# Consecutive weight rows on each partition, and every fourth feature to match, in the expert stage of a hybrid encoder

## The chip, the core and the metric

The kernel runs on one core of one Trainium2 chip. TensorE multiplies matrices, VectorE, ScalarE and GpSimd do the elementwise work, SyncE (SP) issues nearly all DMAs, and 16 DMA engines move the data. The metric is the device time of one execution in microseconds.

## The reference

One encoder layer over 256 tokens of 1024 features in float32: a mixer of three branches (retention, neighbourhood attention, cross attention to a memory), an output projection with a residual, and then a mixture of experts. Only the last part is touched:

```python
t = rmsnorm(x, g_ffn)                      # 256 x 1024
grp = top-1 of 4 groups, exp = top-2 of 4 experts in that group, with weights
for g in range(4):
    a = einsum('td,edf->tef', t, w_gate[g])      # 4 experts, 1024 -> 512
    u = einsum('td,edf->tef', t, w_up[g])
    hid = silu(a) * u * combine[:, g, :, None]
    out += einsum('tef,efd->td', hid, w_down[g]) # 512 -> 1024
y = rmsnorm(x + out, g_final)
```

Each of the 16 experts has 2 MB of gate, 2 MB of up and 2 MB of down weights: some 100 MB, which are read once.

## The kernel before, in words

Ahead of the experts the kernel projects, attends and mixes; TensorE runs products of split pairs (a high and a low part, L128 and L129 make them, L306 to L308 multiply). There a scheduler orders the instructions by its own costs, except those that are pinned in program order (`pin`, `tc.keep_in_program_order`). The small loads for the router stand in this part: its weights `wr` (L727, L728; L730 multiplies them by the gain column `gt[:, 3]`), biases, the constants `iota` and `tri` (L739 casts it) and x. All go through SP's one queue, among the loads of the next weights.

From L796 on the order is written out by hand. The expert weights arrive in slots of 1 MB, [128 partitions, 2048 floats], some 20 of them. `expert_units` makes the list of 96 loads in the order of use. `fetch(tag)` issues the next load into the slot that came free, `take` hands the oldest loaded slot to the matmuls. A load is issued when the last matmul on its slot is done.

The stage runs over 8 pairs of experts; each expert has room for 64 tokens. Every second pair, `gather` picks the tokens of four experts: 32 matmuls, whose stationary operand is a 128-feature slice of the normalised activations (`x1_hi`, then `x1_lo`) and whose moving operand is the 0/1 matrix `pd`. The result, multiplied by the norm gain while it leaves PSUM, is `xg`: feature k*128 + p on partition p of block k. For each expert `gate_up` then takes four slots. Each holds 256 rows of gate (two blocks k) and the same of up, row k*128 + p on partition p, so a row of 512 floats is a run of 2 KB. The matmuls have `xg[:, k]` as stationary and the weights as moving operand, gate into the upper, up into the lower half of a bank. ScalarE and VectorE make `gs` of it (silu times up). `hidden` transposes `gs` in four slices of 128 features, `down` multiplies by the down weights (rows of 1024 floats, runs of 4 KB), `weigh` splits and weighs the result, `scatter` adds it to the tokens' sums in PSUM. The last pair is finished with `down_1`, which takes the down weights by halves of the columns (runs of 2 KB). For the tail, slots that are free by then hold `g_final` and the output.

```python
for h, w in ((0, w_gate), (1024, w_up)):
    rows_in(w[e, r : r + 256])(raw[:, h : h + 1024])       # "(k p) n -> p k n"
```

Of the kernel before, what the change touches and what calls it, by code (L numbers as in the profile page):

```python
# [9 lines left out]
F32 = mybir.dt.float32  # L10
# [4 lines left out]
AF = mybir.ActivationFunctionType  # L15
# [3 lines left out]
P = 128  # L19
T = 256  # L20
D = 1024
KT = D // P
NEG = -1e30
SLOTS = 64
NE = 16
NP = NE // 2
DFF = 512
# [3 lines left out]
def hybrid_encoder_kernel(  # L31
# [31 lines left out]
    nc = tc.nc  # L63
    w_gate = w_gate[0].rearrange("g e d f -> (g e) d f")
    w_up = w_up[0].rearrange("g e d f -> (g e) d f")
    w_down = w_down[0].rearrange("g e f d -> (g e) f d")
    V, A, G, PE = nc.vector, nc.scalar, nc.gpsimd, nc.tensor

    cp = ctx.enter_context(tc.tile_pool(name="cp", bufs=1))
# [19 lines left out]
    pin = tc.keep_in_program_order  # L89
# [18 lines left out]
    def hl_pair(shape):  # L108
        tag = hl_tags.pop(0)
        hl_tags.append(tag)  # L110
        t = slot(tag, [P, 2, *shape], F32R)
        return tag, t[:, 0], t[:, 1]
# [24 lines left out]
    feeder = [nc.sync]  # L137
# [6 lines left out]
        plan.pop(0)(raw)  # L144
        ready.append((tag, raw))

    def rows_in(src, parts=1):
        def go(raw):
            dst = raw.rearrange("p (k n) -> p k n", n=src.shape[1])
            k = dst.shape[1] // parts  # L150
            for i in range(parts):
                feeder[0].dma_start(
                    dst[:, i * k : i * k + k], src[i * k * P : (i + 1) * k * P].rearrange("(k p) n -> p k n", p=P)
                )

        return go

# [15 lines left out]
    gt = cp.tile([P, 4, KT], F32, name="gt")  # L173
# [4 lines left out]
    for q in range(4):  # L178
        rs = slice(q * 256, q * 256 + 256)
# [3 lines left out]
    ident = cp.tile([P, P], F32, name="ident")  # L183
# [72 lines left out]
    with tc.manual_schedule():  # L256
# [4 lines left out]
        for q in range(4):  # L261
            ks = (2 * q, 2 * q + 1)
            gained(xT, 0, hT_hi, hT_lo, ks)
            _, w_hi, w_lo = hl_pair([2, 512])
            for k in ks:
                raw = first[k // 4][:, k % 4]
# [160 lines left out]
    def xa_scores(hp):  # L427
        s = at([P, 4, 256])
        for j in range(2):
            h = 2 * hp + j  # L430
            for a in range(2):
                ts = slice(a * P, (a + 1) * P)
                mm3(s[:, 2 * j + a], xq_hi[:, h, ts], xq_lo[:, h, ts], mk_hi[:, h], mk_lo[:, h], True, True)
        return softmax(s, P ** -0.5)
# [56 lines left out]
    p = xa_scores(0)  # L491
# [11 lines left out]
    def na_scores(hp):  # L503
        sps = at([P, 4, 256])
        for a in range(2):
            ts = slice(a * P, (a + 1) * P)
            for i, (q, k) in enumerate(((nq_hi, nk_hi), (nq_hi, nk_lo), (nq_lo, nk_hi))):
                for j in range(2):
                    rs = slice(j * 64, j * 64 + 64)
                    pin(PE.matmul(sps[:, 2 * j + a], q[rs, hp, ts], k[rs, hp], start=i == 0, stop=i == 2))  # L510
        s = tmp([P, 4, 256])
        mx = tiny(4, tag="mx")
        for j in range(2):
            for a in range(2):
                i = 2 * j + a
                r0 = 2 - 2 * a
                b = bias[2 * hp + j][:, r0 : r0 + 4].rearrange("p r c -> p (r c)")
                V.tensor_tensor_reduce(s[:, i], sps[:, i], b, 0.125, -3e38, ALU.add, ALU.max, accum_out=mx[:, i : i + 1])
        return softmax(s, 1.0, mx)
# [49 lines left out]
    p = na_scores(0)  # L569
    rk_hi, rk_lo = rope_T("C1", proj_T(units_T(W, C_RK, D), hT_hi, hT_lo))  # L570
    ps = na_probs(p)
    p = na_scores(1)
# [13 lines left out]
    p = na_scores(2)  # L586
# [3 lines left out]
    p = na_scores(3)  # L590
# [112 lines left out]
    w = ret_scores(0)  # L703
    rg(0)
    ret_out(0, *w)
    w = ret_scores(1)
# [17 lines left out]
    raw_tags.append("B1")  # L724
    wr = wp.tile([P, KT, 32], F32, tag="gs", name="wr")
    V.memset(wr, 0.0)
    tc.keep_in_program_order(nc.sync.dma_start(wr[:, :, 16:20], w_rg[0].rearrange("(k p) n -> p k n", p=P)))  # L727
    tc.keep_in_program_order(nc.sync.dma_start(wr[:, :, 0:16], w_re[0].rearrange("(k p) n -> p k n", p=P)))  # L728
    for k in range(KT):
# [34 lines left out]
    def expert_units():  # L764
        us = []

        def gate_and_up(e, r):
            def go(raw):
                for h, w in ((0, w_gate), (1024, w_up)):
                    rows_in(w[e, r : r + 256])(raw[:, h : h + 1024])  # L770

            return go

        def gu(e):
            us.extend(gate_and_up(e, r) for r in range(0, D, 256))

        def dn(*es):
            for r in (0, 256):
                us.extend(rows_in(w_down[e, r : r + 256]) for e in es)

        def dn_cols(e):
            for c in (0, 512):
                us.append(rows_in(w_down[e, :, c : c + 512], 2 if c and e == NE - 1 else 1))

        for p in range(NP):
            gu(2 * p)
            if p:
                dn(2 * p - 2, 2 * p - 1)
            gu(2 * p + 1)
        dn_cols(NE - 2)  # L790
        dn_cols(NE - 1)
        return us
# [8 lines left out]
    tag = raw_tags.pop(0)  # L801
# [6 lines left out]
    parts = []  # L808
    for i, (tag, raw) in enumerate(out_raw):
        src = w_out[0, i % 2 * 512 : i % 2 * 512 + 512, i // 2 * 512 : i // 2 * 512 + 512].rearrange("(k p) n -> p k n", p=P)  # L810
        if i < 3:
            nc.sync.dma_start(raw, src)
            raw = [raw[:, :2], raw[:, 2:]]
# [106 lines left out]
    def bank(shape):  # L920
        return psc.tile(shape, F32, tag="b", name=nm("b"))
# [59 lines left out]
    def normed_lo(a, n):  # L981
        ns = slice(n * 512, n * 512 + 512)
        V.scalar_tensor_tensor(
            x1_lo[:, a, ns], x1[:, a, ns], r2[:, a : a + 1], x1_hi[:, a, ns].bitcast(F32), op0=ALU.mult, op1=ALU.subtract
        )
# [130 lines left out]
    def gather(pd, lead=False):  # L1116
        pts = [bank([P, 2, 256]) for _ in range(4)]

        def part(u, x, first):
            for j in range(2):  # L1120
                ks = slice((2 * u + j) * P, (2 * u + j + 1) * P)
                for a in range(2):
                    PE.matmul(
                        pts[u][:, j],
                        x[:, a, ks],
                        pd[:, a].rearrange("p e s -> p (e s)"),
                        start=first and j + a == 0,
                        stop=not first and j + a == 2,
                    )

        if lead:
            for u in range(4):
                part(u, x1_hi, True)
            for n in range(2):
                for a in range(2):
                    normed_lo(a, n)
        xg = slot("C1", [P, KT, 4, SLOTS])
        for u in range(4):
            pt = pts[u]
            if not lead:  # L1140
                part(u, x1_hi, True)
            part(u, x1_lo, False)
            if u % 2:
                for j in range(2):
                    k = 2 * u + j
                    A.activation(
                        xg[:, k].rearrange("p e s -> p (e s)"), pt[:, j], AF.Copy, scale=gt[:, 3, k : k + 1]
                    )
            else:
                V.tensor_tensor(  # L1150
                    xg[:, 2 * u : 2 * u + 2].rearrange("p k e s -> p k (e s)"),
                    pt,
                    gt[:, 3, 2 * u : 2 * u + 2].unsqueeze(2).to_broadcast([P, 2, 256]),
                    op=ALU.mult,
                )
        return xg
# [22 lines left out]
    def take(n):  # L1179
        tag, raw = ready.pop(0)  # L1180
        return tag, raw.rearrange("p (k n) -> p k n", n=n)

    def gate_up(xg, i, p, gs, between=None):
        pt = bank([P, DFF])
        for u in range(2):
            for h in range(2):
                tag, w = take(DFF)
                for j in range(2):
                    k = 4 * u + 2 * h + j
                    for c in range(2):  # L1190
                        PE.matmul(  # L1191
                            pt[c * 64 : c * 64 + 64], xg[:, k, p % 2 * 2 + i], w[:, 2 * c + j], start=k == 0, stop=k == KT - 1
                        )
                fetch(tag)
            if between and not u:
                between()
        gs = gs or keep([P, DFF], "gs")
        A.activation(gs[64:128], pt[0:64], AF.Silu)  # L1198
        V.tensor_mul(gs[i * 64 : i * 64 + 64], gs[64:128], pt[64:128])  # L1199
        return gs  # L1200
# [34 lines left out]
    def hidden(gs, hh=None, i=0):  # L1235
        rs = slice(i * 64, i * 64 + 64) if hh else slice(0, P)
        pt = bank([P, 4, P])
        for j in range(4):
            PE.transpose(pt[:, j, rs], gs[rs, j * P : (j + 1) * P], ident[rs, rs])
        hh = hh or keep([P, 4, P], "hh")  # L1240
        A.copy(hh[:, :, rs], pt[:, :, rs])
        return [hh[:, :, n * 64 : n * 64 + 64] for n in range(2)]
# [43 lines left out]
    def experts(pd, first, lead=False):  # L1286
        st = {}

        def turn():
            st["h"] = hidden(st["gs"])  # L1290
# [135 lines left out]
```

## Time and profile before

| | us |
|---|---|
| median of three runs (545.28 to 545.74) | 545.31 |
| the profiled execution | 545.44 |
| its span in the trace | 543.5 |
| TensorE busy in the span | 528.5 |
| VectorE, ScalarE, GpSimd busy | 264.3, 229.0, 18.5 |

The profile is that of one execution. Its page gives busy times of each engine; a matmul's end in it is modelled, so that pipelined matmuls overlap in the records and their starts say more than their lengths. PE stands for TensorE's matmuls, PEld for its weight loads (the stationary operand), which can run beside a matmul. DVE is VectorE, ACT ScalarE, SPq the queue of SyncE that issues DMAs. In the windows, the first number behind a stretch is its length, then the busy time of each engine with its instructions, the granted clock of TensorE as a share of full speed, the share of time that the 16 DMA engines were busy, and GB/s. The page puts the DMAs at a mean of 294 GB/s over the span, with 89815 packets for 159.91 MB, 89776 of them under 8 KB.

### The profile page before, as it was taken

The numbers are of one execution on the slowest core, as the hardware profiler recorded it, in microseconds if no ns is written. First come the engines' busy times: TensorE is split into PE (matmuls) and PEld (weight loads), VectorE is DVE, ScalarE is ACT, GpSimd is POOL, SyncE is SP. The second block draws the span as 40 slices with busy tenths as digits, with TensorE's granted clock in tenths as the row PEclk, the third lists the DMA queues.
The fourth block names the chain that finished last, engine by engine and source line by source line (L and its number), as shares of the span: only waits on it lengthen the run. The fifth ranks groups of instructions, "written<-read, shape, count | busy, mean of one in ns | idle before, by whom it ended". The sixth has DMA issues, their size and how long they took to land. (4 is left out here: it accounts for less than half of the span.)

```text
span 543.5 us, 7482 instructions
## 1 busy us (share of the span) xinstructions
PE 528.5 (97%) x2912; PEld 359.9 (66%) x2912; DVE 264.3 (49%) x461; ACT 229.0 (42%) x378; POOL 18.5 (3%) x21
## 2 busy tenths in 40 slices
PE   8999999999999999999999999999999999999992
PEld 6999899967778888888888863353435343534340
DVE  6598798995657768384566171130112111210122
ACT  6775566698654464544535261121111111111123
POOL 0005000040000000000000000000000000000000
PEclk9999999999999999999999999999999999999997
DMA  8987778045445799739983799999999999999962
GB/s 302 390 316 233 224 147 256 17 156 163 148 154 189 235 334 301 257 103 403 354 318 151 275 344 330 416 406 418 406 414 409 409 413 407 416 406 418 406 242 81
DMA packets 89815, 159.91 MB, mean 294 GB/s; under 512 B 13104, under 2 KB 27824, under 8 KB 89776
## 3 DMA queue, kind: packets, MB, share of 16 engines
q1 hardware_dynamic: 89056, 158.80, 80.1%
q10 hardware_dynamic: 720, 0.58, 0.3%
q8 instruction: 25, 0.41, 0.3%
q14 instruction: 14, 0.11, 0.1%
HBM read 158.32 MB, written 1.05 MB: 293 GB/s over the span
## 5 line engine op out<-in xcount | busy, mean ns | idle before, releaser
L129 DVE TENSOR_TENSOR h<-r,h 128x1024 fp32r<-128x1024 f32 x58 | 71.2, 1239 | 31.6 <-ACT h L128 31.2
L128 ACT CAST h<-r 128x1024 fp32r<-128x1024 f32 x58 | 60.2, 1048 | 23.4 <-PE pj L308 12.5
L306 PE MATMUL pj<-h,A 128*128 128x512 f32 x160 | 63.1, 394 | 0.0
L308 PE MATMUL pj<-h,A 128*128 128x512 f32 x160 | 62.7, 392 | 0.0
L307 PE MATMUL pj<-h,A 128*128 128x512 f32 x160 | 62.6, 391 | 0.0
L1199 DVE TENSOR_TENSOR gs<-gs,b 64x512 f32<-64x512 f32 x16 | 11.1, 691 | 87.1 <-ACT gs L1198 87.1
L288 PE MATMUL pj<-A,h 128*128 128x256 f32 x160 | 45.7, 286 | 0.0
L290 PE MATMUL pj<-A,h 128*128 128x256 f32 x160 | 45.5, 284 | 0.0
L289 PE MATMUL pj<-A,h 128*128 128x256 f32 x160 | 45.3, 283 | 0.0
L308 PEld LDWEIGHTS pj<-h,A 128*128 128x128 f32 x160 | 30.1, 188 | 6.9 <-issue 0.8
L306 PEld LDWEIGHTS pj<-h,A 128*128 128x128 f32 x160 | 30.1, 188 | 6.7 <-issue 0.4
L307 PEld LDWEIGHTS pj<-h,A 128*128 128x128 f32 x160 | 30.1, 188 | 6.3 <-DVE h L129 0.4
L1230 DVE SCALAR_TENSOR_TENSOR os<-b,c,os 128x512 fp32r<-128x512 f32 x16 | 12.0, 751 | 41.9 <-ACT os L1229 41.0
L1198 ACT ACTIVATE gs<-b 64x512 f32<-64x512 f32 x16 | 9.4, 588 | 51.8 <-PE b L1191 51.8
L288 PEld LDWEIGHTS pj<-A,h 128*128 128x128 f32 x160 | 30.7, 192 | 0.1
L290 PEld LDWEIGHTS pj<-A,h 128*128 128x128 f32 x160 | 30.7, 192 | 0.1
L289 PEld LDWEIGHTS pj<-A,h 128*128 128x128 f32 x160 | 30.7, 192 | 0.1
L129 DVE TENSOR_TENSOR h<-G,h 128x1024 fp32r<-128x1024 f32 x18 | 24.1, 1346 | 10.3 <-ACT h L128 9.8
L1229 ACT ACTIVATE os<-b,c 128x512 fp32r<-128x512 f32 x16 | 11.0, 687 | 40.6 <-PE b L1210 39.7
L1191 PE MATMUL b<-h,C 128*64 128x512 f32 x104 | 24.0, 592 | 0.0
L128 ACT CAST h<-G 128x1024 fp32r<-128x1024 f32 x18 | 18.8, 1049 | 10.6 <-PE pj L308 9.3
L1210 PE MATMUL b<-h,hh 128*64 128x512 f32 x64 | 21.3, 592 | 0.0
(327 smaller groups left out, 1029.3 us busy)
## 6 DMA issues: line engine op xcount, KB each, us to landing
r<-in_w_in_dram SPq DMA_DIRECT2D x20, 1024.0 KB, 5.4
h<-in_w_exp_down_dram SPq DMA_DIRECT2D x10, 1024.0 KB, 11.5
h<-in_w_exp_gate_dram SPq DMA_DIRECT2D x13, 512.0 KB, 11.0
h<-in_w_exp_up_dram SPq DMA_DIRECT2D x13, 512.0 KB, 11.1
r<-in_w_exp_down_dram SPq DMA_DIRECT2D x6, 1024.0 KB, 11.6
A<-in_w_exp_down_dram SPq DMA_DIRECT2D x5, 1024.0 KB, 11.4
r<-in_w_exp_gate_dram SPq DMA_DIRECT2D x9, 512.0 KB, 10.2
r<-in_w_exp_up_dram SPq DMA_DIRECT2D x9, 512.0 KB, 10.3
```

What stands on the lines that cost most here:

```text
L128: pin(A.copy(hi, part))
L129: pin(V.tensor_sub(lo, part, hi.bitcast(F32)))
L288: PE.matmul(pt, whi[:, cs], thi[:, k], start=k == 0, stop=False)
L289: PE.matmul(pt, whi[:, cs], tlo[:, k], start=False, stop=False)
L290: PE.matmul(pt, wlo[:, cs], thi[:, k], start=False, stop=k == kn - 1)
L306: PE.matmul(pts[a], thi[:, kk, ts], whi, start=first, stop=False)
L307: PE.matmul(pts[a], thi[:, kk, ts], wlo, start=False, stop=False)
L308: PE.matmul(pts[a], tlo[:, kk, ts], whi, start=False, stop=last)
L1191: PE.matmul(pt[c * 64 : c * 64 + 64], xg[:, k, p % 2 * 2 + i], w[:, 2 * c + j], start=k == 0, stop=k == KT - 1)
L1199: V.tensor_mul(gs[i * 64 : i * 64 + 64], gs[64:128], pt[64:128])
L1210: PE.matmul(pts[n][i * 64 : i * 64 + 64], hh[:, 2 * u + k], ws[i][1][:, k, ns], start=u + k == 0, stop=u + k == 2)
L1230: V.scalar_tensor_tensor(o[:, 1], pt, c, o[:, 0].bitcast(F32), op0=ALU.mult, op1=ALU.subtract)
```

## The change

The features get another order within the expert stage. Each half of 512 rows is laid on the partitions so that partition p holds the four rows 4p to 4p+3, one run of 8 KB for gate and for up; a slot now holds 512 rows of gate alone or of up alone, loaded by one DMA. For the down weights partition p holds rows 4p to 4p+3 as well, and a slot two of them (8 KB). To match, the gather takes every fourth feature as its stationary operand, the transposes in `hidden` take every fourth column of `gs`, and the norm gain comes from a new tile `gx` that eight small DMAs fill in the new order, issued from SP ahead of the router weights. `gate_up` takes the gate and the up slot together, works through four blocks k, and only then frees both.

```diff
@@ -144,14 +144,12 @@
         plan.pop(0)(raw)
         ready.append((tag, raw))
 
-    def rows_in(src, parts=1):
+    def runs_in(src, parts=1):
         def go(raw):
-            dst = raw.rearrange("p (k n) -> p k n", n=src.shape[1])
+            dst = raw.rearrange("p (k n) -> p k n", n=src.shape[2])
             k = dst.shape[1] // parts
-            for i in range(parts):
-                feeder[0].dma_start(
-                    dst[:, i * k : i * k + k], src[i * k * P : (i + 1) * k * P].rearrange("(k p) n -> p k n", p=P)
-                )
+            for i in range(0, dst.shape[1], k):
+                feeder[0].dma_start(dst[:, i : i + k], src[:, i : i + k])
 
         return go
 
@@ -724,6 +722,11 @@
     raw_tags.append("B1")
     wr = wp.tile([P, KT, 32], F32, tag="gs", name="wr")
     V.memset(wr, 0.0)
+    gx = cp.tile([P, KT], F32, name="gx")
+    for q in range(4):
+        src = gains.rearrange("(p j) c -> p j c", j=4)
+        for u in range(2):
+            pin(nc.sync.dma_start(gx[q * 32 : q * 32 + 32, 4 * u : 4 * u + 4], src[:, :, 24 + 4 * u + q]))
     tc.keep_in_program_order(nc.sync.dma_start(wr[:, :, 16:20], w_rg[0].rearrange("(k p) n -> p k n", p=P)))
     tc.keep_in_program_order(nc.sync.dma_start(wr[:, :, 0:16], w_re[0].rearrange("(k p) n -> p k n", p=P)))
     for k in range(KT):
@@ -764,23 +767,20 @@
     def expert_units():
         us = []
 
-        def gate_and_up(e, r):
-            def go(raw):
-                for h, w in ((0, w_gate), (1024, w_up)):
-                    rows_in(w[e, r : r + 256])(raw[:, h : h + 1024])
-
-            return go
-
         def gu(e):
-            us.extend(gate_and_up(e, r) for r in range(0, D, 256))
+            for r in (0, 512):
+                us.extend(runs_in(w[e, r : r + 512].rearrange("(p j) n -> p j n", j=4)) for w in (w_gate, w_up))
+
+        def by_four(e):
+            return w_down[e].rearrange("(p k) n -> p k n", k=4)
 
         def dn(*es):
-            for r in (0, 256):
-                us.extend(rows_in(w_down[e, r : r + 256]) for e in es)
+            for k in (0, 2):
+                us.extend(runs_in(by_four(e)[:, k : k + 2]) for e in es)
 
         def dn_cols(e):
             for c in (0, 512):
-                us.append(rows_in(w_down[e, :, c : c + 512], 2 if c and e == NE - 1 else 1))
+                us.append(runs_in(by_four(e)[:, :, c : c + 512], 2 if c and e == NE - 1 else 1))
 
         for p in range(NP):
             gu(2 * p)
@@ -1118,7 +1118,8 @@
 
         def part(u, x, first):
             for j in range(2):
-                ks = slice((2 * u + j) * P, (2 * u + j + 1) * P)
+                k = 2 * u + j
+                ks = slice(k // 4 * 512 + k % 4, k // 4 * 512 + 512, 4)
                 for a in range(2):
                     PE.matmul(
                         pts[u][:, j],
@@ -1144,13 +1145,13 @@
                 for j in range(2):
                     k = 2 * u + j
                     A.activation(
-                        xg[:, k].rearrange("p e s -> p (e s)"), pt[:, j], AF.Copy, scale=gt[:, 3, k : k + 1]
+                        xg[:, k].rearrange("p e s -> p (e s)"), pt[:, j], AF.Copy, scale=gx[:, k : k + 1]
                     )
             else:
                 V.tensor_tensor(
                     xg[:, 2 * u : 2 * u + 2].rearrange("p k e s -> p k (e s)"),
                     pt,
-                    gt[:, 3, 2 * u : 2 * u + 2].unsqueeze(2).to_broadcast([P, 2, 256]),
+                    gx[:, 2 * u : 2 * u + 2].unsqueeze(2).to_broadcast([P, 2, 256]),
                     op=ALU.mult,
                 )
         return xg
@@ -1183,14 +1184,13 @@
     def gate_up(xg, i, p, gs, between=None):
         pt = bank([P, DFF])
         for u in range(2):
-            for h in range(2):
-                tag, w = take(DFF)
-                for j in range(2):
-                    k = 4 * u + 2 * h + j
-                    for c in range(2):
-                        PE.matmul(
-                            pt[c * 64 : c * 64 + 64], xg[:, k, p % 2 * 2 + i], w[:, 2 * c + j], start=k == 0, stop=k == KT - 1
-                        )
+            ws = [take(DFF) for _ in range(2)]
+            for k in range(4 * u, 4 * u + 4):
+                for c in range(2):
+                    PE.matmul(
+                        pt[c * 64 : c * 64 + 64], xg[:, k, p % 2 * 2 + i], ws[c][1][:, k % 4], start=k == 0, stop=k == KT - 1
+                    )
+            for tag, _ in ws:
                 fetch(tag)
             if between and not u:
                 between()
@@ -1236,7 +1236,7 @@
         rs = slice(i * 64, i * 64 + 64) if hh else slice(0, P)
         pt = bank([P, 4, P])
         for j in range(4):
-            PE.transpose(pt[:, j, rs], gs[rs, j * P : (j + 1) * P], ident[rs, rs])
+            PE.transpose(pt[:, j, rs], gs[rs, j::4], ident[rs, rs])
         hh = hh or keep([P, 4, P], "hh")
         A.copy(hh[:, :, rs], pt[:, :, rs])
         return [hh[:, :, n * 64 : n * 64 + 64] for n in range(2)]
```

## Rows read from the trace of the kernel before

**Rows 1.** The page: busy time of each engine, its share of the span, and instructions.

```profile
PE 528.5 (97%) x2912; PEld 359.9 (66%) x2912; DVE 264.3 (49%) x461; ACT 229.0 (42%) x378; POOL 18.5 (3%) x21
```

**Rows 2.** Windows: length, busy times PE, PEld, DVE, ACT, POOL, clock, DMA share, GB/s.

```profile
270.00:280.00 10.00, 10.00 (x49) 8.08 (x48) 6.95 (x9) 2.96 (x4) 0.00 (x0) 1.00 1.00 378
420.00:430.00 10.00, 10.00 (x50) 3.40 (x48) 0.69 (x1) 1.40 (x3) 0.00 (x0) 1.00 1.05 406
430.00:440.00 10.00, 10.00 (x56) 4.34 (x54) 1.50 (x2) 1.37 (x2) 0.00 (x0) 1.00 1.03 420
330.00:520.00 190.00, 190.00 (x994) 78.77 (x992) 30.32 (x64) 31.19 (x58) 0.00 (x0) 1.00 1.04 409
```

**Rows 3.** Waits from 330 to 530: who waited for whom, us in total, times, longest.

```profile
PEld b L1210 <- DMA T<-in_w_exp_gate_dram: 0.6, 2, 0.3
...
PEld b L1191 <- DMA E<-in_w_exp_gate_dram: 0.3, 1, 0.3
```

**Rows 4.** Timeline of TensorE, 505 to 544: start, us, instruction, count.

```profile
510.45 1.94 PE L1191 MATMUL b<-G,C 128*64 128x512 f32 x8
512.21 1.89 PE L1191 MATMUL b<-h,C 128*64 128x512 f32 x8
```

**Rows 5.** Timeline of SP's queue, 489 to 506.

```profile
494.11 4.77 SPq L152 DMA_DIRECT2D h<-in_w_exp_up_dram  x1
```

**Rows 6.** DMAs issued from 488 to 516: count, KB each, median us to landing.

```profile
h<-in_w_exp_up_dram SPq DMA_DIRECT2D x1, 512.0 KB, 15.1
```

**Rows 7.** Timeline of SP's queue, 317 to 331.

```profile
317.79 0.48 SPq L152 DMA_DIRECT2D T<-in_w_exp_up_dram  x1
326.45 0.37 SPq L152 DMA_DIRECT2D B<-in_w_exp_gate_dram  x1
```

**Rows 8.** Timeline of TensorE, 319 to 330.

```profile
324.48 1.94 PE L1191 MATMUL b<-B,C 128*64 128x512 f32 x8
326.24 1.89 PE L1191 MATMUL b<-E,C 128*64 128x512 f32 x8
```

**Rows 9.** Timeline of TensorE, 413 to 426.

```profile
416.31 0.64 PE L1123 MATMUL b<-X,C 128*128 128x256 f32 x4
416.79 0.64 PE L1123 MATMUL b<-X,E 128*128 128x256 f32 x4
...
422.87 0.66 PE L1239 MATMUL b<-ident,gs 128*128 128x128 f32 x4
```

**Rows 10.** Timeline of TensorE, 207 to 209.

```profile
206.67 0.39 PE L306 MATMUL pj<-h,B 128*128 128x512 f32 x1
206.90 0.39 PE L307 MATMUL pj<-h,B 128*128 128x512 f32 x1
```

**Rows 11.** Weight loads by line and form, 300 to 545: busy us, mean ns.

```profile
L1123 PEld LDWEIGHTS b<-X,E 128*128 128x128 f32 x64 | 8.6, 192 | 0.0
...
L1191 PEld LDWEIGHTS b<-h,C 128*64 128x64 f32 x104 | 7.5, 137 | 14.8 <-issue 14.0 <-PE b L1210 0.9
...
L1239 PEld LDWEIGHTS b<-ident,gs 128*128 128x128 f32 x28 | 2.9, 140 | 5.7 <-issue 5.7
```

**Rows 12.** Timeline of SP's queue, 165 to 262.

```profile
201.24 3.82 SPq L732 DMA_DIRECT2D rb<-in_b_router_group_dram  x1
...
206.05 0.43 SPq L738 DMA_DIRECT2D t<-in_const_tri_dram  x1
...
208.91 0.37 SPq L121 DMA_DIRECT2D B<-in_w_in_dram  x1
```

**Rows 13.** Timeline of VectorE, 202 to 222.

```profile
208.30 0.22 DVE L739 CAST tri<-t 128x128 bf16<-128x128 f32 x1
208.69 1.23 DVE L129 TENSOR_TENSOR h<-C,h 128x1024 fp32r<-128x1024 f32 x1 [0.17 <-ACT h L128]
```

**Rows 14.** DMAs of the whole run, the row of tri.

```profile
t<-in_const_tri_dram SPq DMA_DIRECT2D x1, 64.0 KB, 2.0
```

**Rows 15.** Timeline of ScalarE, 230 to 234.

```profile
232.19 1.04 ACT L128 CAST h<-B 128x1024 fp32r<-128x1024 f32 x1
```

## The prediction

> **What bounds the kernel now.** The page comes first: TensorE is busy for 528.5 of 543.5 us, no other engine for more than half [rows 1]. That is an average, so the next view is the windows of the expert stage, the only stage whose weights the change lays out anew. From 330 to 520 us TensorE is busy for all 190.00 us, at granted clock 1.00 (the higher of its two levels, 2.4 GHz), and in the same time the DMA engines are full too, at a share of 1.04 and 409 GB/s [rows 2]. Two resources look like the bound, and these views can't say which is. Two more can.
>
> The waits: of 200 us before 530, TensorE's weight loads spend 0.6 us in two pieces and 0.3 us in one waiting for a DMA, and that is all [rows 3]. TensorE does not wait for weights.
>
> The timeline says how far it is from waiting. The second slot of expert 14 (tile h) was issued until 494.11 and landed 15.1 us later, at 509.2; its first matmul runs at 512.21, 3.0 us after [rows 4 to 6]. At the stage's start the DMAs are far ahead instead: from 318.3 to 326.45 nothing is issued at all, since all 20 slots are full [rows 7]. So the DMA engines carry weights more slowly than TensorE eats them, and the stock runs down until it is almost used up when the work ends. TensorE sets the end; the DMAs are late by nothing, with 3 us to spare.
>
> **The change part by part.**
>
> *Longer runs.* A gate or up run grows from 2 KB to 8 KB, a down run from 4 KB to 8 KB (two rows that follow each other). The nearest rows: the stretch 420 to 430, with 2 KB runs, moves 406 GB/s; 430 to 440, mostly 4 KB runs, 420; the lowest row at full share is 378 (270 to 280, 2 KB runs of several matrices) [rows 2]. I take 420, the row nearest to a longer run. A slot of 1.0486 MB then takes 2.50 us in place of 2.58. Of the 76 slots issued after the first release, 48 are gate or up: 48 x 0.086 = 4.1 us earlier at the end. On the path that is worth 0: TensorE, which waits for no weights, hides it. At 378 GB/s it would be 48 x 0.19 = 9.2 us later, less the margin.
>
> *Pairs of slots.* A group of matmuls now takes the gate slot and the up slot together, so the first release moves from the end of four matmuls to the end of eight. The first slot's matmuls start at 324.48, the second's at 326.24 [rows 8], and the first refill followed at 326.45 [rows 7]. Refills thus start 1.8 us later, and a second slot is needed 0.2 us after the first, not 1.8. At the tightest place: landing 509.2 + 1.8 = 511.0, wanted at 510.45 + 0.2 [rows 4]. TensorE would wait 0.4 us at the old rate, and nothing with 4.1 us in hand. Cost: 0; the ends are 0 and 0.4 + 9.2 = 9.6 us at 378 GB/s. The number of matmuls and their order over k stay, as do the tail's 2 KB column slots. That 64 slots come by one DMA in place of two relieves only SP, whose issue sets no end: 0.
>
> *Every fourth feature in the gather.* Here the path is touched. The 128 weight loads of L1123 read x1_hi and x1_lo at a step of four floats (16 bytes) in place of one. No row shows TensorE reading at a step. Four matmuls of the gather start every 0.48 us, 120 ns each [rows 9]; a matmul of 512 columns repeats every 230 ns in the projections [rows 10], so 256 columns need some 115. The loads have a cover of about 5 ns here, and what they grow beyond that shows in the end. Load time by columns: 137 ns for 64, 192 for 128 [rows 11], so 64 more columns are 55 ns and 128 stream for 110. Bounds: 0 (the same 128 columns are read, which excludes a gain), and the stream at half its rate, 128 x 110 ns = 14.1 us. The nearest row is that of the transposes: 128 columns in 140 ns [rows 11], about 58 of it streaming, so the read side can hand over columns twice as fast as a gather load takes them. A read that the step halves would still feed the gather at its present pace. I take 0.
>
> The row says that the loads have reserve; a rule speaks against it. The Trainium skill (SBUF — State Buffer, section Door 1: The DMA port swizzle) says that SBUF has lines of 16 bytes, that full rate needs at least two hits in a line, and yet that a step of 4 fp32 is free. A step of 16 bytes has one hit a line: by the first half of that the sum would be up to 14.1 us, by the second 0, and no run shown here decides between them.
>
> *Every fourth feature in the transposes.* 36 loads of L1239 (28 whole, 8 of half height) take the step as well, and these already stream at the faster pace. Bounds: 0, and twice the stream, 36 x 58 ns = 2.1 us. Four transposes span 0.66 us [rows 9], 165 ns each, more than twice their load's stream of 58: I take 0.
>
> *The gain column gx.* Eight small DMAs of 128 four-byte pieces enter SP's queue ahead of the router weights. A small DMA there takes 0.43 us of SP, and 3.82 where the queue was full behind 2048 small pieces [rows 12]: 8 x 0.43 = 3.4 us as I take it (most neighbours show it), 31 at worst. Everything behind them on SP is as much later: the router weights, the biases, the constants, x, the next weights. On VectorE, L730 waits for the router weights and L739 for the constant tri: 206.05 + 3.4 + 2.0 to land = 211.5, where L739 ran at 208.30 [rows 12 to 14], a stall of 3.2 us. Behind it stands the split of the next weights, L129 at 208.69. Four of the five split pairs are then ahead of TensorE, with 12 matmuls of 0.23 us each: 11.0 us (an estimate from [rows 10]), less 2.3 us for that pair's own cast and split, leaves a cover of 8.7. The weights B, issued at 208.91, are cast at 232.19 [rows 12, 15]. Cost 0; the worst end is 31 - 8.9 = 22 us, if each of the eight meets a full queue.
>
> The sum is 0. The profiled execution took 545.44 us (its span 543.5 and 1.9 around it), the median is 545.31. Forecast: 545.4.
>
> **The rivals.**
>
> *Loads at half pace (slower).* One hit in a line halves the stream of the stationary reads. Price: 14.1 in the gathers and 2.1 in the transposes, 545.4 + 16.2 = 561.6. It decides from the point where a stepped load takes over 5 ns more than the 192 of now. For it: the loads are back to back in the gather. Against: the 140 ns of the transposes. Its partial form, in which only the fast transposes and some 15 ns of a gather load show (128 x 15 = 1.9), ends at 547 to 549.
>
> *The DMAs become the bound (slower).* 0.4 us if 8 KB runs are no faster, 9.6 at 378 GB/s: 546 to 555. For it: only 3.0 us of margin. Against: 420 over 406 where runs were longer.
>
> *The small DMAs stall VectorE (slower).* 547 to 550, if they take 11 to 14 us of SP. Against: the 0.43 us of their neighbours.
>
> *The DMAs already are the bound (faster).* Then the 4.1 us come off: 541.3. For it: a share of 1.04. Against: 0.9 us of waits for DMAs in 200.
>
> *The runs are cut to 2 KB again.* Nothing but the later refills is left: 545.8.
>
> **How the numbers follow.** Forecast, 545.4 (own range 544.6 to 546.4): 0.48, and the last rival, with nearly the same time, 0.02. Half pace: 0.25. Its partial form: 0.12. DMAs late: 0.05. VectorE stalled: 0.04. Faster: 0.04. Runs of this kernel can tell about 0.2%, 1.1 us, from no change. Faster by more: 0.04. Within: 0.48 + 0.02 = 0.50. Slower: 0.25 + 0.12 + 0.05 + 0.04 = 0.46. The range goes from 544.4 to 561.6, the full price of half pace; left out are the faster rival and the worst end of the small DMAs.
>
> **What would show it.** Right: matmuls of L1123 still 120 ns apart with loads at 192; 8 KB slots above 409 GB/s; no DMA waits at L1191; first refill near 328. Wrong: loads of L1123 near 300 ns and a gather of 7 us in place of 4; or DMA waits at L1191; or TensorE idle near 215 us, behind L739.

## The result, and the profile after

The changed kernel is slower. Its median is 563.12 us (562.40 to 563.73, four runs) beside 545.52 for the kernel before in the same session: 17.6 us more, a ratio of 1.0323 [1.031, 1.0336]. The forecast was 545.4, the rival of loads at half pace 561.6, which was also the end of the range; the time lies 1.5 us beyond it. The profiled execution took 563.73 us, its span 561.6.

The page of after: busy time, share and instructions, and the DMA line.

```profile
PE 544.5 (97%) x2912; PEld 377.6 (67%) x2912; DVE 263.2 (47%) x461; ACT 229.2 (41%) x378; POOL 18.5 (3%) x21
DMA packets 61783, 159.91 MB, mean 285 GB/s; under 512 B 13232, under 2 KB 27952, under 8 KB 49968
```

TensorE has as many matmuls as before and is busy 16.0 us longer, its loads 17.7 us [rows 1]. So most of the 18.1 us that the span grew is work that became longer, and only some 2 us are a wait that appeared. Where the work became longer is seen in two views. The timeline of TensorE at the first gather:

```profile
322.79 4.18 PE L1124 MATMUL b<-X,C 128*128 128x256 f32 x16 [0.83 <-DVE X L1108]
326.77 3.87 PE L1124 MATMUL b<-X,E 128*128 128x256 f32 x16
330.57 0.64 PE L1190 MATMUL b<-B,C 128*64 128x512 f32 x1
```

The gather begins at 322.79 and gate's first matmul at 330.57: 7.78 us for 32 matmuls, 243 ns each. Weight loads by line and form, with busy us and mean ns:

```profile
L1124 PEld LDWEIGHTS b<-X,E 128*128 128x128 f32 x64 | 16.2, 330 | 0.0
...
L1190 PEld LDWEIGHTS b<-h,C 128*64 128x64 f32 x104 | 11.8, 137 | 11.4 <-issue 10.6 <-PE b L1210 0.9
...
L1239 PEld LDWEIGHTS b<-ident,gs 128*128 128x128 f32 x28 | 3.9, 208 | 5.7 <-issue 5.7
```

Against [rows 11], both groups that read at a step are longer, 192 to 330 ns and 140 to 208, and the gate loads beside them, which have no step, take the same 137.

Windows of after (length; busy PE, PEld, DVE, ACT, POOL; granted clock; DMA share; GB/s):

```profile
20.00:28.00 8.00, 8.00 (x69) 8.00 (x68) 3.61 (x5) 4.95 (x8) 0.71 (x1) 1.00 1.10 346
31.90:35.30 3.40, 3.40 (x14) 3.22 (x15) 2.19 (x4) 1.13 (x3) 0.00 (x0) 0.50 1.09 353
325.50:328.90 3.40, 3.40 (x16) 3.40 (x16) 0.82 (x2) 0.01 (x1) 0.00 (x0) 0.50 0.34 145
330.00:520.00 190.00, 190.00 (x915) 85.58 (x916) 28.23 (x60) 29.05 (x54) 0.00 (x0) 1.00 0.98 406
530.00:540.00 10.00, 10.00 (x72) 4.83 (x70) 0.65 (x3) 1.33 (x3) 0.00 (x0) 1.00 0.00 0
```

The last two lines say that the weights are no part of it. In 330 to 520 the DMA engines are less full than before (0.98, [rows 2] has 1.04), and from 530 to 540 they move nothing at all while TensorE still works. From 330 to 520 TensorE waits for no DMA.

The first line is a surprise: at 20 us, long before any expert, where the diff touches nothing, the DMAs move 346 GB/s. The same window of the kernel before:

```profile
20.00:28.00 8.00, 8.00 (x69) 8.00 (x69) 3.94 (x6) 6.16 (x9) 0.72 (x1) 1.00 1.09 381
```

**The sum.** Both kernels issue 2912 matmuls; how much later the nth starts in after than in before gives a lag at every place. It is 2.5 to 2.9 us from 32 us on and 2.5 from 60 us until the gather. It rises to 6.1 with the first gather, by 14.5 over the four (113 ns for each of 128 matmuls, which start every 233 ns in place of 120), and by 1.1 over the 36 transposes, to 18.17 at the last matmul. The spans differ by 18.1. So three things are to be explained: the gathers (14.5), the transposes (1.1) and the start (2.5).

### The profile page after: what moved, and what is told of

The parts are those of the page before. It is cut to its first block, busy times and chain, and to the rows that moved or that the text cites. A ratio compares the mean times of both kernels' runs of the same rounds, so it can differ in the third digit from the quotient of the medians.

```text
span 561.6 us, 7415 instructions
## 1 busy us (share of the span) xinstructions
PE 544.5 (97%) x2912; PEld 377.6 (67%) x2912; DVE 263.2 (47%) x461; ACT 229.2 (41%) x378; POOL 18.5 (3%) x21
## 5 line engine op out<-in xcount | busy, mean ns | idle before, releaser
L286 PE MATMUL pj<-A,h 128*128 128x256 f32 x160 | 46.4, 290 | 0.0
L288 PE MATMUL pj<-A,h 128*128 128x256 f32 x160 | 46.0, 288 | 0.0
L287 PE MATMUL pj<-A,h 128*128 128x256 f32 x160 | 45.8, 286 | 0.0
L1190 PE MATMUL b<-h,C 128*64 128x512 f32 x104 | 39.6, 594 | 0.0
L286 PEld LDWEIGHTS pj<-A,h 128*128 128x128 f32 x160 | 31.4, 196 | 0.1
L287 PEld LDWEIGHTS pj<-A,h 128*128 128x128 f32 x160 | 31.2, 195 | 0.1
L288 PEld LDWEIGHTS pj<-A,h 128*128 128x128 f32 x160 | 31.2, 195 | 0.1
L1190 PE MATMUL b<-B,C 128*64 128x512 f32 x64 | 29.0, 596 | 0.0
L1190 PE MATMUL b<-G,C 128*64 128x512 f32 x64 | 29.0, 596 | 0.0
## 6 DMA issues: line engine op xcount, KB each, us to landing
h<-in_w_exp_up_dram SPq DMA_DIRECT2D x8, 1024.0 KB, 17.7
r<-in_w_exp_down_dram SPq DMA_DIRECT2D x6, 1024.0 KB, 15.7
```

The source lines that it names most:

```text
L286: PE.matmul(pt, whi[:, cs], thi[:, k], start=k == 0, stop=False)
L287: PE.matmul(pt, whi[:, cs], tlo[:, k], start=False, stop=False)
L288: PE.matmul(pt, wlo[:, cs], thi[:, k], start=False, stop=k == kn - 1)
L1190: PE.matmul(pt[c * 64 : c * 64 + 64], xg[:, k, p % 2 * 2 + i], ws[c][1][:, k % 4], start=k == 0, stop=k == KT - 1)
```

## The experiments

Two theories for the gathers: either the step slows the loads, or the transfers do, since slots now come and go in pairs with 8 KB runs. For the start, the one thing that the change adds in SBUF is the tile `gx`, 32 bytes on each partition, and everything allocated behind it should move by that (the traces show no addresses).

**The gather's step alone.** The kernel before, with its own weight layout, takes every fourth feature in the gather and nothing else.

```diff
-                ks = slice((2 * u + j) * P, (2 * u + j + 1) * P)
+                k = 2 * u + j
+                ks = slice(k // 4 * 512 + k % 4, k // 4 * 512 + 512, 4)
```

> The kernel before with one edit: the gather's stationary slices take every fourth feature (so it gathers features in another order than the weights have). Theory (stepped weight loads): the 128 loads go from 192 to about 330 ns, each gather from 4.2 to 7.8 us, 4 x 3.65 = 14.6 us, so about 560.1 us. Rival (the 8 KB slots, taken in pairs, cost the time): nothing changes, 545.5 us. Rival (the eight small DMAs cost 2.5 us at the start): no start loss here, so not above 560.5.

Measured: 559.92 us, ratio 1.0265 [1.0247, 1.0282], +14.7. One line's rows of this kernel: count, min/median/max ns, first and last start.

```profile
L1124 PEld LDWEIGHTS b<-X,E x64: 329/329/333, 324.5 to 485.9; 128*128 128x128 f32 x64
L1124 PE MATMUL b<-X,E x64: 350/396/441, 324.7 to 486.0; 128*128 128x256 f32 x64
```

The lag is 0.41 ahead of the gathers and 14.90 at the end: 14.5, with no new layout, no pairs and no `gx`. The step is the cause.

**The gather without it.** After, with the gather's slices as they were.

```diff
-                ks = slice(k // 4 * 512 + k % 4, k // 4 * 512 + 512, 4)
+                ks = slice(k * P, (k + 1) * P)
```

> The changed kernel with the gather's slices contiguous again (features then don't match the weights' order); slots, small DMAs and transposes stay as changed. Theory: 563.1 - 14.6 = 548.5 us, or 546.5 if the 2.5 us at the start belong to some runs only. Rival (pairs of slots, 8 KB runs): stays at 563.

Measured: 548.65 us, ratio 1.0059 [1.004, 1.0077]. The lag is 2.67 before and after the first gather; 3.5 us by the medians are left, which the gather doesn't make.

**The transposes without it.**

```diff
-            PE.transpose(pt[:, j, rs], gs[rs, j::4], ident[rs, rs])
+            PE.transpose(pt[:, j, rs], gs[rs, j * P : (j + 1) * P], ident[rs, rs])
```

> The changed kernel with the transposes' slices contiguous again (hidden features then don't match the down weights' order). Theory: the 36 loads go from 209 back to 140 ns, worth 1.0 us (from the timelines) to 2.5 us (36 x 69 ns): 560.6 to 562.1 us. Rival (transposes hidden behind other work): 563.1.

Measured: 561.43 us, ratio 1.0301 [1.0281, 1.0322], 1.7 less than after.

```profile
L1239 PEld LDWEIGHTS b<-ident,gs x36: 135/140/143, 347.6 to 538.8; 128*128 128x128 f32 x28, 64*128 64x128 f32 x8
```

The loads are at 140 ns again. Its lag grows by 14.53 over the expert stage, where after's grows by 15.7: the transposes account for 1.1 of the 1.7. The rest lies in the start, whose lag differs from one profiled execution to another (1.4 here; the reason is below, with the place of the tiles).

**Other steps.** After with a gather that takes every second or every eighth feature:

```diff
+                ks = slice(k // 2 * 256 + k % 2, k // 2 * 256 + 256, 2)      # one kernel
+                ks = slice(k, D, 8)                                          # the other
```

> The changed kernel with a step of 2 floats (8 bytes) in the gather in place of 4 (features then don't match). If a load slows only when each element lies in a line of its own (one hit in 16 bytes), loads are back at 192 ns and the time is about 548.5 us. If the slowing grows with the bytes spanned, loads are near 240 to 260 ns and the time 552 to 556 us. If any step other than one costs the same, 330 ns and 563.1 us.

> The changed kernel with a step of 8 floats (32 bytes) in the gather in place of 4 (features then don't match the weights' order). If a load slows because each element lies in another line of 16 bytes, a step of 8 is no worse: 330 ns and 563.1 us. If the slowing grows with the bytes spanned, loads take some 600 ns and the time is near 595 us.

Measured: step 2, 548.79 us, 1.0067 [1.0044, 1.0089]; step 8, 564.66 us, 1.035 [1.0332, 1.0368] (two runs). The loads at step 2, and then at step 8 (busy us, mean ns):

```profile
L1124 PEld LDWEIGHTS b<-X,E x64: 194/195/196, 323.9 to 473.2; 128*128 128x128 f32 x64
```

```profile
L1124 PEld LDWEIGHTS b<-X,E 128*128 128x128 f32 x64 | 16.7, 338 | 0.0
```

Contiguous 192, step 2 195, step 4 330, step 8 338 ns: the price hardly grows with the step, but jumps between steps of 8 and 16 bytes, where two neighbouring reads no longer share 16 bytes. This agrees with what the Trainium skill (SBUF — State Buffer, section Door 1: The DMA port swizzle) says of lines and hits. The same section calls a step of 4 fp32 free; for these reads of TensorE the rows say otherwise, and they decide. The mechanism itself is not seen in any trace, and the transposes' loads at step 2, further below, do not follow it.

**The moving operand at a step.** The kernel before, with the weights of gate and up, the moving operand, read at a step of four floats.

```diff
-                            pt[c * 64 : c * 64 + 64], xg[:, k, p % 2 * 2 + i], w[:, 2 * c + j], start=k == 0, stop=k == KT - 1
+                            w.rearrange("p k n -> p (k n)").rearrange("p (n k) -> p k n", k=4)[:, 2 * c + j], ...
```

> The kernel before with the moving operand of the gate and up matmuls read at a step of four floats (weights are then mixed up); stationary reads as before. If the line of 16 bytes slows moving reads as it slows weight loads, the 512 matmuls of L1191, 214 ns each, double: 545 + 110 = 655 us. If moving reads have reserve enough, 545.3 us.

Measured: 665.42 us, ratio 1.2205 [1.2182, 1.2227] (two runs). The matmuls of this kernel, and then of the kernel before:

```profile
L1191 PE MATMUL b<-h,C x104: 1057/1079/1083, 357.5 to 629.3; 128*64 128x512 f32 x104
```

```profile
L1191 PE MATMUL b<-h,C x104: 592/592/593, 340.7 to 513.5; 128*64 128x512 f32 x104
```

A matmul's record is 1079 ns long in place of 592, and the starts come every 450 ns on average in place of 214. So a step of four floats about halves the pace on both sides, and costs 120 us where the larger operand has it.

**The order made at the writes.** All of the new layout stays, but `x1_hi`, `x1_lo` and `gs` are written in the new order by ScalarE and VectorE, which read at the step, and TensorE reads contiguously. (`gx` has 64 bytes here.)

```diff
-        A.activation(x1_hi[:, a, ns], x1[:, a, ns], AF.Copy, scale=r2[:, a : a + 1])
+        A.activation(by_p(x1_hi[:, a, ns]), by_j(x1[:, a, ns]), AF.Copy, scale=r2[:, a : a + 1])
...
-            PE.transpose(pt[:, j, rs], gs[rs, j::4], ident[rs, rs])
+            PE.transpose(pt[:, j, rs], gs[rs, j * P : (j + 1) * P], ident[rs, rs])
```

> The changed kernel with gx as in e6 and the order of the features made where x1_hi, x1_lo and gs are written: ScalarE and VectorE read at a step of four floats and write every tile in the order of the weights, so that all of TensorE's slices are contiguous. Same result as the reference. Theory: gather loads at 192 ns, transposes' at 140, time as before, 545.2 us, plus up to 0.5 us for eight stepped elementwise operations near 320 us. Rival (8 KB runs or pairs of slots cost something of their own): above 546.5. Rival (faster DMAs are worth something): below 544.2.

Measured: 549.10 us, ratio 1.0069 [1.0057, 1.0081]; the expected time was missed by 3.4 us. The trace is that of the fastest of six executions (548.21 us) and places 2.5 of them; three of the six, at a mean granted clock of 0.989 to 0.991 in place of 0.994 for the fastest, took 549.6 to 549.9 us. The lag is 1.24 at the end of the projections and still at the first gather matmul, 2.50 at the first gate matmul, and then within 0.05 of that to the end. The first part is the start. The second is VectorE's write of `x1_lo`, for which TensorE stops in the middle of the first gather. ScalarE's write of `x1_hi` grew too, but in time in which ScalarE waited before: the gather begins no later for it. The stop, VectorE's write in this kernel and in the kernel before, and ScalarE's in the two:

```profile
325.95 1.10 PE L1135 MATMUL b<-X,E 128*128 128x256 f32 x7 [0.64 <-DVE E L989]
```

```profile
L989 DVE SCALAR_TENSOR_TENSOR E<-C,r,C x4: 1104/1124/1162, 321.6 to 324.8; 128x512 fp32r<-128x512 f32 x4
```

```profile
L983 DVE SCALAR_TENSOR_TENSOR E<-C,r,C x4: 746/748/748, 320.4 to 322.4; 128x512 fp32r<-128x512 f32 x4
```

```profile
L985 ACT ACTIVATE C<-C,r x4: 1196/1206/1217, 315.8 to 319.1; 128x512 fp32r<-128x512 f32 x4
```

```profile
L979 ACT ACTIVATE C<-C,r x4: 713/715/731, 314.6 to 316.4; 128x512 fp32r<-128x512 f32 x4
```

The flat lag says the most: over the whole expert stage, 8 KB runs, one DMA a slot and slots in pairs cost nothing on TensorE's path and give nothing.

**The place of the tiles.** Four kernels. Before with a tile of 32 bytes that nothing reads, before with one of 512; after with `gx` made 64 bytes long, after with 512.

```diff
+    spare = cp.tile([P, KT], F32, name="spare")           # before, 32 bytes; the other: 16 * KT
...
+    gx = cp.tile([P, 2 * KT], F32, name="gx")[:, :KT]     # after, 64 bytes; the other: 16 * KT
```

> The kernel before with one tile more in the constants' pool, 8 floats (32 bytes) a partition, cleared once and never read; nothing else. Theory (place in SBUF): the 32 bytes of gx move every later tile, and DMAs with 1 KB runs into tiles so moved carry 346 GB/s in place of 380 in 20 to 28 us; TensorE then waits near 30 us: 545.2 + 1.5 to 2.7 = 546.7 to 547.9 us. Rival (the eight small DMAs, or the other order of the weights' loads, slow the start): 545.2 us and 380 GB/s.

> The changed kernel with gx held in a tile of 64 bytes a partition in place of 32 (its second half unused), so that later tiles move by 64 bytes. Theory (place in SBUF): 380 GB/s again in 20 to 28 us, TensorE's 60 x 3rd matmul at its old time, 563.1 - 2.0 = 561.1 us (560.4 to 561.6). Rival (small DMAs, loads' order): 563.1 us and 346 GB/s.

> The changed kernel with gx held in a tile of 512 bytes a partition (its first 32 in use). Theory (place in SBUF, steps of 512 bytes): every later tile again begins at a multiple of 512 bytes, as before; 380 GB/s in 20 to 28 us, no wait of TensorE near 30 us, 563.1 - 1.2 to 2.7 = 560.4 to 561.9 us. Rival (the start is slowed by something else of the change): 563.1 us and 346 GB/s.

> The kernel before with an unused tile of 512 bytes a partition in the constants' pool (e5 had 32). Theory (place, multiples of 512 bytes): 545.4 us, 380 GB/s in 20 to 28 us and 406 to 412 in the expert stage. Rival (any move of the tiles, or the tile's clearing, costs): 554 us as e5.

| kernel | us | ratio | GB/s at 20:28 (1 KB runs) | GB/s at 370:420 (before: 2 and 4 KB runs, after: 8 KB) |
|---|---|---|---|---|
| before | 545.2 to 545.5 | | 381 | 412 |
| before, 32 bytes | 553.88 | 1.0149 [1.0134, 1.0163] | 346 | 396 |
| before, 512 bytes | 545.39 | 1.0001 [0.9991, 1.001] | 381 | 412 |
| after (32 bytes) | 563.12 | 1.0323 [1.031, 1.0336] | 346 | 419 |
| after, 64 bytes | 563.35 | 1.0323 [1.0308, 1.0338] | 347 | 421 |
| after, 512 bytes | 561.01 | 1.0292 [1.0277, 1.0307] | 381 | 427 |

The windows of before with 32 bytes, and then with 512:

```profile
20.00:28.00 8.00, 8.00 (x69) 8.00 (x68) 3.33 (x5) 4.88 (x7) 0.72 (x1) 1.00 1.09 346
370.00:420.00 50.00, 50.00 (x252) 19.82 (x251) 7.04 (x13) 7.86 (x14) 0.00 (x0) 1.00 1.04 396
```

```profile
20.00:28.00 8.00, 8.00 (x69) 8.00 (x69) 3.39 (x5) 5.78 (x8) 0.71 (x1) 1.00 1.09 381
370.00:420.00 50.00, 50.00 (x261) 21.24 (x258) 8.13 (x14) 7.96 (x15) 0.00 (x0) 1.00 1.04 412
```

The share is the same and the rate isn't: each transfer takes longer where the tiles behind moved by 32 or 64 bytes, and not where they moved by 512. The traces' packet records say how much: some 3 to 5 ns a packet from 1 to 8 KB (medians: 1 KB 46 to 51 ns, 2 KB 84 to 87, 4 KB 159 to 164, 8 KB 309 to 313), which is why short runs lose most. The 561.1 us expected with 64 bytes were thus wrong. With 512 the lag of after is 0.08 at the end of the projections in place of 2.5, and the median falls by 2.1.

How a slower DMA reaches the path at the start is seen in the waits of after from 15 to 45 us (total, times, longest), where the kernel before has 0.4 us for the first pair and 0.3 for the second, each in one piece:

```profile
ACT h L128 <- DMA r<-in_w_in_dram: 1.6, 2, 1.1
PEld at L237 <- DVE t L232: 2.2, 1, 2.2
```

ScalarE's cast waits for the late tile, VectorE's half of that split comes behind it, and behind that, on VectorE, the small diagonal matrix of L232, for which TensorE pauses 2.2 us. Right behind that pause the clock is granted at 0.50, the 1.2 GHz level, for 3.4 us (the window 31.90:35.30 above). With 64 bytes the profiled execution shows the pause (TensorE busy 2.52 of the 4 us from 31) without that drop and a lag of 1.9. Of the eight profiled executions whose tiles moved by 32 or 64 bytes, the four with such a drop between 32 and 37 us lag by 2.5 to 3.0 us behind the start, the four without by 1.2 to 1.9. So the wait is worth 1.2 to 1.9 us, and the drop, which follows it in some executions, about 1 us more.

What was not foreseen is the end of the kernel before with 32 bytes: 8.4 us slower, of which 3.0 are the start. The waits of TensorE (loads and matmuls, which overlap) on DMAs in its expert stage, the three largest:

```profile
PEld b L1212 <- DMA r<-in_w_exp_down_dram: 4.9, 3, 2.3
PE b L1212 <- DMA r<-in_w_exp_down_dram: 2.9, 2, 1.5
PE b L1223 <- DMA A<-in_w_exp_down_dram: 0.5, 1, 0.5
```

The lag is 2.98 until 500 us and 8.85 at the end: at 387 to 396 GB/s the stock of slots runs out and the DMAs do become the bound. After has no such wait, but its TensorE is 15 us later and gives the DMAs more time. The better witness is the kernel with the order made at the writes: 64 bytes, 8 KB runs at 421 GB/s, a flat lag, and a single wait of TensorE for a DMA, of 0.2 us.

**Two rows on each partition.** The layout cut to step 2: gate and up in runs of 4 KB, down of 8 KB, step 2 in gather and transposes, `gx` of 512 bytes.

```diff
-                us.extend(runs_in(w[e, r : r + 512].rearrange("(p j) n -> p j n", j=4)) for w in (w_gate, w_up))
+                us.extend(runs_in(w[e, r : r + 512].rearrange("(c p j) n -> p c (j n)", c=2, j=2)) for w in (w_gate, w_up))
...
+                ks = slice(k // 2 * 256 + k % 2, k // 2 * 256 + 256, 2)
...
-            PE.transpose(pt[:, j, rs], gs[rs, j::4], ident[rs, rs])
+            PE.transpose(pt[:, j, rs], gs[rs, j // 2 * 256 + j % 2 : j // 2 * 256 + 256 : 2], ident[rs, rs])
```

> The change with two consecutive rows a partition in place of four: runs of 4 KB for gate and up, 8 KB for down, the gather and the transposes take every second feature, gx in 512 bytes. Same result as the reference. Theory: a step of 8 bytes loads at 195 ns and the place in SBUF is that of before, so TensorE's path is as before: 545.3 us (544.6 to 546.2). Rival (pairs of slots, small DMAs, later refills cost something): above 546.5. Rival (faster DMAs are worth something): below 544.2.

Measured: 547.34 us, ratio 1.0034 [1.0022, 1.0047], where 545.3 was expected. Gather and transposes of this kernel:

```profile
L1131 PEld LDWEIGHTS b<-X,E x64: 194/195/196, 322.4 to 471.7; 128*128 128x128 f32 x64
```

```profile
L1246 PEld LDWEIGHTS b<-ident,gs x36: 192/209/218, 342.6 to 524.0; 128*128 128x128 f32 x28, 64*128 64x128 f32 x8
```

The gather is free, but the transposes' loads go to 209 ns at step 2 just as at step 4. The lag is 0.06 behind the first gather and 1.18 at the last matmul: the transposes' 1.1 again. Some 0.8 us of the 1.95 between the two profiled executions lies outside the matmuls and was not followed. No version beat the kernel before.

## Why the prediction was wrong

**Right.** TensorE sets the end, and faster transfers are worth nothing: the flat lag of the order made at the writes. The pairs cost nothing: the first refill is issued 3.68 us behind the first gate matmul in place of 1.97, 1.7 us later where 1.8 was taken, and no wait follows. 8 KB runs are faster (419 to 427 GB/s; 420 was taken). The small DMAs cost nothing on the path, though they took 7.9 us of SP's queue and not 3.4: the lag is 2.53 ahead of them and 2.51 behind. The cover of 8.7 was hardly tried, though. The router's loads behind them went into the queue faster (0.58 us for the one that had taken 3.82), so the load of B was issued at 213.39 in place of 208.91, only 2.0 us more than the lag. Two slips carry no weight: 494.11 is where the issue of h's second load begins, not where it ends [rows 5] (the landing at 509.2 counts from there), and the worst end of the small DMAs takes 8.9 off where the cover was 8.7.

**The step that failed: "Every fourth feature in the gather".** It had the price, the stream at half its rate, 14.1 us, and the runs show 14.5. It had the sign as well: loads near 300 ns and a gather of 7 us, where 330 and 7.8 came. It took 0, because of the transposes' row: 128 columns in 140 ns [rows 11], read as a reserve of the read side that a step could use up. That row shows no step. It tells how fast another form reads contiguously, not that a gather load is limited by something other than its reads. The gather loads went from 192 to 330 ns, and the matmuls that they pace came 113 ns further apart, about the 110 of the stream: none of the supposed reserve took it up. The right reading of the rows was that the loads stand back to back with a cover of 5 ns, and that nothing shown excluded the full price: a cost of 0 needed a row, the price didn't. The rival had a chance of 0.25 where the evidence for the two was about even.

**"Every fourth feature in the transposes. I take 0."** Four transposes took 0.66 us, more than twice their stream, and that was to hide the longer loads. The loads grew by 36 x 69 ns = 2.5 us, and 1.1 of it shows at the end; the cover was there, but for half of it.

**"The gain column gx. Cost 0."** Its queue was priced and its place was not: 32 bytes that move every tile behind them cost 2.1 us by the medians (after against 512 bytes; 1.7 by their ratios to the kernel before, which come from two sessions), 2.5 in the profiled execution, all in the first 35 us. No view of the kernel before shows that. This is why the time lies beyond the rival's: 545.4 + 14.5 + 1.1 + 2.1 = 563.1. Without the place, at 512 bytes, it is 561.0 beside the rival's 561.6; that is in part luck, since the rival took 0.4 us too little for the gathers and 1.0 too much for the transposes.

## What to carry to other kernels

A layout that makes transfers longer puts its step on the reader, so price the reader's side first: here TensorE was the bound and the DMAs had nothing to give. An fp32 operand of TensorE, stationary or moving, should not be read at a step of four floats; eight cost the stationary one as much, and two were free in the gather, not in the transposes. After adding a small tile, compare the GB/s of an untouched stretch, and pad it to 512 bytes if the rate fell.

## What the runs showed of the hardware

- TensorE's pace about halves at a step of 16 bytes, for the gather's stationary and for the gate and up matmuls' moving operand: gather loads 192 to 330 ns, with a matmul every 233 ns in place of 120; matmuls of 512 moving columns every 450 ns in place of 214. ScalarE pays as well for a read at that step (715 to 1206 ns for 512 columns), and so does VectorE (748 to 1124 ns for the other of the two writes).
- The transposes' loads take 140 ns contiguous and 209 at step 2 and step 4 alike, while gather loads take 195 and 330. Why the two forms differ stays open.
- Tiles that moved by 32 or 64 bytes took DMAs at 346 GB/s in place of 381, and 419 in place of 427 with 8 KB runs; 512 bytes made no difference. The loss is some 3 to 5 ns a packet, at 1 KB as at 8 KB. Which offset between 64 and 512 would do wasn't tried, nor which tile matters.
- In the first gather of after the granted clock is 0.50, the 1.2 GHz level, from 325.5 to 328.9; what TensorE did before was 2.7 us of the same stepped loads. That gather cost 3.6 us, as each of the others did, and 3.55 with 512 bytes, where the clock stayed at 1.00: while its loads are the limit, the clock of the matmuls cost nothing that shows. The drop behind the pause at the start, with no stepped loads, did cost about 1 us.
